# Dilated scores of a head pair on the two row halves of the TensorE array, three products of 64 rows each, instead of two stacked products of 128 rows

## The chip, the cores and the metric

The kernel runs on one core of a Trainium2 chip. A core has a matrix engine (TensorE, called PE in the profile; its weight loads are listed apart as PEld), a vector engine (DVE), a scalar engine (ACT), a general engine (POOL) and a queue engine that issues most transfers (SP). Each engine works through its own instructions in the order in which the program lists them, and they wait for one another by semaphores. The metric is the device time of one execution in microseconds (us), smaller being better; the number of a version is the median of several executions.

## What is computed

Two layers of an encoder over 1024 tokens of width 1024. Layer 0 is latent attention, layer 1 is dilated window attention; each is followed by an MLP. The change touches the dilated attention alone: 16 heads of 64 dimensions in three groups with (window, dilation) of (128, 1), (512, 4) and (2048, 16). For each group and head the reference does this:

```python
q = rms_norm(proj[:, :, gi, 0], g_q[gi])
k = rms_norm(proj[:, :, gi, 1], g_k[gi])
...
s = jnp.einsum('nbqhd,nbkhd->nbhqk', qb, kb,
               preferred_element_type=jnp.float32) * (DIL_HEAD_DIM ** -0.5) + bias
s = jnp.where(valid[None, :, None], s, -jnp.inf)
lse = jax.nn.logsumexp(s, axis=-1)
p = jnp.exp(s - lse[..., None]).astype(v.dtype)
o = jnp.einsum('nbhqk,nbkhd->nbqhd', p, vb)
```

The scores s of a block of 128 queries against its 256 neighbouring keys are a product over 64 dimensions. The kernel makes float32 accuracy out of a shorter format (F32R in the code): every operand is split into a high part and a remainder, hi and lo, and the product becomes a sum of products of parts.

## The kernel before

The dilated stage (function `dil`) walks through steps of 128-row tile pairs: for each of three groups g and eight head pairs pr, four steps tp, each of which takes two tiles of 128 tokens. A loop at the end of `dil` calls the parts of a software pipeline in turn. In one step it projects the tile pair tp (`project`, 24 products of 128x256 for each tile, on the lines 414 to 416 of the helper `mm3`), normalizes it (`qkstep`), transposes an earlier pair and splits it into hi and lo (`stacks`), computes scores for two tiles that are ready (`scores`), transposes the weights of two earlier tiles (`ptrans`) and multiplies two others with the values (`av`). Program order is only the starting point: the framework simulates the program and writes each engine's list in the order in which its model of durations finds the instructions ready.

`stacks` (L1832) transposes the queries and keys of both heads into one PSUM bank psq: 128 rows, 64 of each head. For head e it then writes a stack into the tile kT: hi on the head's own 64 rows (ACT, L1846) and lo on the other 64 rows (DVE, L1847). The tile has one such 128-row plane for each head. For the queries it needs the stack in swapped order too, lo above hi, and gets it by two transfers on SP's queue into the tile qs (L1850).

`scores` (L1860) thus needs two products of all 128 rows for a head: stack times stack gives hi·hi + lo·lo, swapped stack times stack gives lo·hi + hi·lo. That is four products of 128x256 for the two heads of a tile (L1873), all into the two halves of one PSUM bank pss. DVE adds the bias tile bt and takes the row maximum (L1878, once a head), ACT makes the offset dnb (L1882) and the exponential into the tile pd (L1884). The PSUM pool of the stage has eight banks, handed out in turn.

Before the stage there is one place to which the prediction turns: the table of bias values is built with nine products of only 32 rows (L1444, in the function `bias_even`), and the latent attention multiplies weights with values on L870 to L872, with 66, 64 and 66 columns of the array.

Of the kernel before, what the change touches and what calls it, by code (L numbers as in the profile page):

```python
# [9 lines left out]
F32 = mybir.dt.float32  # L10
F32R = mybir.dt.float32r
# [3 lines left out]
AF = mybir.ActivationFunctionType  # L15
ALU = mybir.AluOpType
# [4 lines left out]
P = 128  # L21
D = 1024
S = 1024
# [18 lines left out]
class K:  # L42
# [1702 lines left out]
    def dil(self, at0, at1, tail, wqk, vd):  # L1745


        nc, a, tc = self.nc, self.a, self.tc
# [4 lines left out]
        D_ = lambda name, shape, dt, bufs: dpool.tile(list(shape), dt, tag=name, bufs=bufs, name=self.nm(name))  # L1753
        PS = lambda name, dt=F32: psp.tile([P, 512], dt, tag="b", name=self.nm(name))
# [12 lines left out]
        def project(h, w, ps, i, t):  # L1767
            tl = slice((t % 4) * P, (t % 4 + 1) * P)
            for d in range(ND):
                self.mm3(ps[:, i * 256 : (i + 1) * 256], h[t // 4](0, d)[:, tl], h[t // 4](1, d)[:, tl],  # L1770
                         w[d // 4][0][:, d % 4, :], w[d // 4][1][:, d % 4, :], d == 0, d == ND - 1)
# [60 lines left out]
        def stacks(u, tp, qn):  # L1832

            ps = PS("psq")
            for k in range(2):
                for i in range(2):
                    c = i * 256 + (1 - k) * P
                    nc.tensor.transpose(ps[:, (2 * k + i) * P : (2 * k + i + 1) * P], qn[:, c : c + P], self.ident)
            q0 = S + tp % 2 * 256
            qs = D_("qs", (P, 2, 256), F32R, 3)  # L1840
            for e in range(2):
                n, m = (slice(64 * x, 64 * x + 64) for x in (e, 1 - e))
                s1 = 4 + tp % 2
                pair = lambda r: u["k"][r, e, :].rearrange("p (s x) -> p s x", x=256)[:, tp : s1 + 1 : s1 - tp, :]
                x = ps[n, :].rearrange("p (k x) -> p k x", k=2)
                nc.scalar.activation(pair(n), x, AF.Copy)  # L1846
                nc.vector.tensor_tensor(pair(m), x, pair(n).bitcast(F32), op=ALU.subtract)  # L1847
            for r in range(2):
                n, m = (slice(64 * x, 64 * x + 64) for x in (r, 1 - r))
                nc.sync.dma_start(out=qs[n].bitcast(F32), in_=u["k"][m, :, q0 : q0 + 256].bitcast(F32))  # L1850
            for i in range(2):
                u["q"][2 * tp + i] = (u["k"][:, :, q0 + i * P : q0 + (i + 1) * P], qs[:, :, i * P : (i + 1) * P])

        def span(g, t):
            if g == 2:
                return 64, 192
            n = 8 if g == 0 else 2
            return 64 if t % n == 0 else 0, 192 if t % n == n - 1 else 256

        def scores(u, t):  # L1860
            g, pr = u["g"], u["pr"]
            bt = D_("bt", (P, 2, 256), F32, 3)
            idx = self.even * (8 - t) + t
            src = self.bias[g][bass.ds(idx, 1), 2 * pr : 2 * pr + 2, 0 : P * 256]
            b0, b1 = (64, 192) if g == 2 else (0, 256)
            nc.sync.dma_start(out=bt[:, :, b0:b1], in_=src.rearrange("o h (q c) -> q (o h) c", c=256)[:, :, b0:b1])
            ps = PS("pss")
            w0 = min(max(P * t - 64, 0), S - 256)
            off = w0 - (P * t - 64)
            q = u["q"].pop(t)  # L1870
            for e in range(2):
                for k in range(2):
                    nc.tensor.matmul(ps[:, e * 256 : (e + 1) * 256], q[k][:, e, :], u["k"][:, e, w0 : w0 + 256],  # L1873
                                     start=k == 0, stop=k == 1)
            lo, hi = span(g, t)
            p = D_("pd", (P, 2, 256), F32, 4)
            for e in range(2):
                nc.vector.tensor_tensor_reduce(  # L1878
                    p[:, e, lo:hi], ps[:, e * 256 + lo - off : e * 256 + hi - off], bt[:, e, lo:hi], op0=ALU.add, op1=ALU.max,
                    scale=1.0, scalar=-3.0e38, accum_out=stat[:, g, t, 0, 2 * pr + e : 2 * pr + e + 1])  # L1880
            nb = self.sm("dnb", 2)
            nc.scalar.activation(nb, stat[:, g, t, 0, 2 * pr : 2 * pr + 2], AF.Identity, scale=-1.0, bias=ln14)  # L1882
            for e in range(2):
                nc.scalar.activation(p[:, e, lo:hi], p[:, e, lo:hi], AF.Exp, bias=nb[:, e : e + 1],  # L1884
                                     accum_out=stat[:, g, t, 1, 2 * pr + e : 2 * pr + e + 1])
            if g < 2:
                if lo:
                    nc.gpsimd.memset(p[:, :, 0:lo], 0)
                if hi < 256:
                    nc.gpsimd.memset(p[:, :, hi:256], 0)  # L1890
            return p
# [138 lines left out]
        def fetch(n):  # L2030
            if n in firsts:
                loads[n] = self.dil_weights(*firsts[n][1:3])

        def fetch_split(n):
            if n in firsts:
                wts[firsts[n][0:3]] = loads.pop(n)()
# [43 lines left out]
        transposed, scored, ready, carry, stacking, stk, late, after = [], [], [], [], None, [], [], None  # L2080
# [6 lines left out]
        for n, step in enumerate(steps):  # L2087
            fetch(n + 2)
            for f in vtodo.pop(n, ()):
                f()  # L2090
            if step is None and perms:
                while perms:
                    permute(*perms.pop(0))
                HT = new
                h = [(lambda k, d, t=t: t[k][d // 2][:, d % 2, :]) for t in HT]
            if step is not None and n + 1 < len(steps) and steps[n + 1] is None and step[1] < 2:
                new = [[[], []], [[], []]]
                perms = [(step[1] + 1, dp, k) for dp in range(4) for k in range(2)]
                for _ in range(2):
                    permute(*perms.pop(0))  # L2100
            w = None
            if step is not None:
                kind, g, pr, tp = step
                w = wts[(kind, g, pr)]
                if tp == 0:
                    units[(g, pr)] = {"g": g, "pr": pr, "q": {}, "V": VSs[(g, pr // 2)],
                                      "k": D_("kT", (P, 2, S + 512), F32R, 2), "U": self.G("U", (P, 8, P), F32)}
                u = units[(g, pr)]
            for x in transposed:
                x[0]["at"] = n  # L2110
                av(*x)
            fetch_split(n + 1)
            if step is not None:
                ps = PS("psproj")
                project(h, w, ps, 0, 2 * tp)
            transposed = [(u_, t_, ptrans(u_, t_, p_)) for u_, t_, p_ in scored]
            for u_, t_, _ in scored:
                if u_["g"] == 2:
                    if u_["pr"] < 7:
                        if t_ == 7:  # L2120
                            um(u_, (0, 1))
                    elif t_ in (1, 5):
                        um(u_, (t_ // 4,))
            scored = [(u_, t_, scores(u_, t_)) for u_, t_ in ready]
            ready, carry = carry, []
            stk.append(stacking)
            if len(stk) > 1:
                x = stk.pop(0)
                if x is not None:
                    stacks(*x)  # L2130
                    u_, tp_ = x[:2]
                    ready = ready + ([(u_, 2 * tp_ - 1), (u_, 2 * tp_)] if tp_ else [(u_, 0)])
                    carry = [(u_, 7)] if tp_ == 3 else []
            late, merged[:] = late + merged, []
            while late and (step is None or late[0][1] < n):
                u_, _, ths = late.pop(0)
                emit(u_, ths)
            if step is not None:
                project(h, w, ps, 1, 2 * tp + 1)
                if step == ("qk", 2, 7, 3):  # L2140
                    tail()
                    after = n + 1
            if n == after:
                for pp in range(3):
                    self.reload(O, src, pp, 0, nc.sync)
            stacking = None
            if step is not None:
                stacking = (u, tp, qkstep(u, tp, ps))
# [163 lines left out]
```

## Time and profile before

| | us |
|---|---|
| median of 3 executions | 3348.64 |
| lowest and highest | 3348.17, 3349.63 |
| the profiled execution, its own time | 3350.56 |
| span of its instructions | 3348.8 |
| first and last product of L1873 in the span | 1692.2 to 2618.2 |

The mean granted TensorE clock was 0.981. A row of the timeline gives an instruction's start and its duration, both in us from the start of the span; a group row gives count, busy time and mean duration in ns, and then the idle time of that engine just before these instructions with what ended it. Products overlap: a product of 128x256 is listed with some 0.28 us though the next one starts 0.12 us later. So the engine's pace is read from the distance of the starts, not from the durations, and a busy PE need not be at its best pace.

### The profile page before, as it was taken

What the parts mean: (1) busy time and instruction counts of PE and PEld (TensorE: products, weight loads), DVE (VectorE), ACT (ScalarE), POOL (GpSimd) and SP (SyncE); (2) the same over time, 40 slices, a digit from 0 to 9 for tenths busy, and PEclk for the clock granted to TensorE, in tenths of its full rate; (3) what the DMA queues carried; (4) which work ended last, traced back from release to release, by engine and by line L of the source; (5) the groups of instructions that cost most, each with busy time, mean ns of one, the idle gap of its engine ahead of it and who ended that gap; (6) DMA issues with size and microseconds to landing.
All of it is one profiled execution on the core that took longest, in us unless ns stands there. A gap on an engine that the chain in (4) does not pass through costs nothing. (4 is left out here: it accounts for less than half of the span.)

```text
span 3348.8 us, 52027 instructions
## 1 busy us (share of the span) xinstructions
PE 3201.8 (96%) x18278; PEld 2737.9 (82%) x18278; DVE 2521.1 (75%) x4491; ACT 1810.8 (54%) x3606; POOL 749.9 (22%) x1077
## 2 busy tenths in 40 slices
PE   6999999999999999899999989998898899999999
PEld 6877677678888788778899989998888688887887
DVE  5677777747877856787678888888899578778666
ACT  5547777735444434542257776677566245444342
POOL 6455565520111000001122222222111001110000
PEclk9999999999999999999999999999999799999999
DMA  5453232243655797546445545544455725439564
GB/s 186 130 170 96 91 103 84 86 157 108 214 185 188 263 283 233 168 143 206 166 121 143 139 125 143 150 133 128 131 146 150 225 85 198 154 128 320 199 198 129
DMA packets 412948, 536.39 MB, mean 160 GB/s; under 512 B 40677, under 2 KB 295058, under 8 KB 412682
## 3 DMA queue, kind: packets, MB, share of 16 engines
q1 hardware_dynamic: 385322, 441.70, 43.2%
q0 software_dynamic: 27360, 91.31, 7.3%
q8 instruction: 146, 2.39, 0.3%
q14 instruction: 120, 0.98, 0.1%
HBM read 376.17 MB, written 132.62 MB: 152 GB/s over the span
## 5 line engine op out<-in xcount | busy, mean ns | idle before, releaser
L415 PE MATMUL psm<-dl,dh 128*128 128x512 f32 x896 | 351.0, 392 | 9.2 <-DVE dl L122 9.1
L414 PE MATMUL psm<-hf,wf 128*128 128x512 f32 x896 | 349.6, 390 | 2.6 <-ACT wf L121 2.5
L416 PE MATMUL psm<-dh,dl 128*128 128x512 f32 x896 | 350.2, 391 | 0.0
L415 PE MATMUL psm<-hf,wf 128*128 128x512 f32 x896 | 348.8, 389 | 0.0
L416 PE MATMUL psm<-hf,wf 128*128 128x512 f32 x896 | 346.7, 389 | 0.4 <-DVE wf L122 0.4
L414 PE MATMUL psm<-dh,dh 128*128 128x512 f32 x896 | 335.1, 391 | 6.1 <-ACT dh L121 6.1
L414 PE MATMUL psproj<-wqkh,hTp 128*128 128x256 f32 x1024 | 301.4, 294 | 1.6 <-DVE stat L1878 1.6
L416 PE MATMUL psproj<-wqkh,hTp 128*128 128x256 f32 x1024 | 291.8, 285 | 0.0
L415 PE MATMUL psproj<-wqkl,hTp 128*128 128x256 f32 x1024 | 291.1, 284 | 0.0
L1829 POOL TENSOR_TENSOR qn<-qn,dgain 128x256 f32<-128x256 f32 x96 | 83.5, 870 | 596.0 <-DVE qn L1827 494.2
L121 ACT ACTIVATE dh<-ufr 128x1024 fp32r<-128x1024 f32 x112 | 118.3, 1056 | 178.5 <-PE psm L416 59.9
L415 PEld LDWEIGHTS psm<-dl,dh 128*128 128x128 f32 x896 | 169.3, 189 | 47.3 <-DVE dl L122 12.0
L414 PEld LDWEIGHTS psm<-dh,dh 128*128 128x128 f32 x896 | 168.2, 188 | 43.1 <-ACT dh L121 8.4
L414 PEld LDWEIGHTS psm<-hf,wf 128*128 128x128 f32 x896 | 168.2, 188 | 39.8 <-ACT wf L121 5.5
L414 PEld LDWEIGHTS psproj<-wqkh,hTp 128*128 128x128 f32 x1024 | 196.4, 192 | 1.9 <-issue 1.9
L416 PEld LDWEIGHTS psm<-hf,wf 128*128 128x128 f32 x896 | 168.2, 188 | 36.2 <-DVE wf L122 1.2
L416 PEld LDWEIGHTS psm<-dh,dl 128*128 128x128 f32 x896 | 169.1, 189 | 35.1
L415 PEld LDWEIGHTS psproj<-wqkl,hTp 128*128 128x128 f32 x1024 | 196.7, 192 | 0.0
L415 PEld LDWEIGHTS psm<-hf,wf 128*128 128x128 f32 x896 | 168.2, 188 | 34.4
L416 PEld LDWEIGHTS psproj<-wqkh,hTp 128*128 128x128 f32 x1024 | 196.2, 192 | 0.0
L122 DVE TENSOR_TENSOR dl<-ufr,dh 128x1024 fp32r<-128x1024 f32 x112 | 136.9, 1222 | 76.5 <-ACT dh L121 57.7
L745 DVE TENSOR_REDUCE mx<-pmx 128x1 f32<-128x512 f32 x256 | 165.1, 682 | 29.5 <-PE pmx L743 29.4
(397 smaller groups left out, 9398.9 us busy)
## 6 DMA issues: line engine op xcount, KB each, us to landing
ufr<-uf SPq DMA_DIRECT2D x112, 512.0 KB
adaw<-in_ada_w SPq DMA_DIRECT2D x96, 512.0 KB
w2r<-in_mlp_w SPq DMA_DIRECT2D x96, 512.0 KB
w1r<-in_mlp_w SPq DMA_DIRECT2D x64, 512.0 KB
bt<-bias SPq DMA_DIRECT2D x128, 256.0 KB
wqkr<-in_dil_w_in SPq DMA_DIRECT2D x96, 256.0 KB
qs<-kT SPq DMA_DIRECT2D x192, 128.0 KB
qkv<-st SPq DMA_DIRECT2D x32, 512.0 KB
```

What stands on the lines that cost most here:

```text
L121: nc.scalar.activation(hi, src, AF.Copy)
L122: (lo_eng or nc.vector).tensor_tensor(lo, src, hi.bitcast(F32), op=ALU.subtract)
L414: mm(out, lh, rh, start=first, stop=False)
L415: mm(out, lh, rl, start=False, stop=False)
L416: mm(out, ll, rh, start=False, stop=last)
L745: nc.vector.tensor_reduce(maxes[h][:, 2 * j + b : 2 * j + b + 1], ps, op=ALU.max, axis=AX.X)
L1829: nc.gpsimd.tensor_tensor(qq, qq, gain[:, g : g + 1, :].unsqueeze(1).broadcast_to([P, 2, 2, 64]), op=ALU.mult)
```

## The change

Queries and keys of both heads are split in place: plane 0 of kT holds hi and plane 1 holds lo, each with head 0 on rows 0 to 63 and head 1 on rows 64 to 127. One ACT and one DVE instruction of 128 rows do it where there were two of 64 rows each; the tile qs and its two transfers are gone. The scores of a head are then three products of 64 rows (hi·hi, lo·hi, hi·lo; lo·lo is left out), on the half of the array's rows on which the head lies. The code lists them in turn, one of head 0, one of head 1. The two heads go to two PSUM banks; the two tiles of a step share these, each in its half of the columns.

```diff
@@ stacks
-            q0 = S + tp % 2 * 256
-            qs = D_("qs", (P, 2, 256), F32R, 3)
-            for e in range(2):
-                n, m = (slice(64 * x, 64 * x + 64) for x in (e, 1 - e))
-                s1 = 4 + tp % 2
-                pair = lambda r: u["k"][r, e, :].rearrange("p (s x) -> p s x", x=256)[:, tp : s1 + 1 : s1 - tp, :]
-                x = ps[n, :].rearrange("p (k x) -> p k x", k=2)
-                nc.scalar.activation(pair(n), x, AF.Copy)
-                nc.vector.tensor_tensor(pair(m), x, pair(n).bitcast(F32), op=ALU.subtract)
-            for r in range(2):
-                n, m = (slice(64 * x, 64 * x + 64) for x in (r, 1 - r))
-                nc.sync.dma_start(out=qs[n].bitcast(F32), in_=u["k"][m, :, q0 : q0 + 256].bitcast(F32))
+            s1 = 4 + tp % 2
+            hi, lo = (u["k"][:, k, :].rearrange("p (s x) -> p s x", x=256)[:, tp : s1 + 1 : s1 - tp, :] for k in range(2))
+            x = ps.rearrange("p (k x) -> p k x", k=2)
+            nc.scalar.activation(hi, x, AF.Copy)
+            nc.vector.tensor_tensor(lo, x, hi.bitcast(F32), op=ALU.subtract)
             for i in range(2):
-                u["q"][2 * tp + i] = (u["k"][:, :, q0 + i * P : q0 + (i + 1) * P], qs[:, :, i * P : (i + 1) * P])
+                c = S + (tp % 2 * 2 + i) * P
+                u["q"][2 * tp + i] = u["k"][:, :, c : c + P]
@@ scores
-        def scores(u, t):
+        def scores(u, t, pss, i):
...
-            ps = PS("pss")
...
-            for e in range(2):
-                for k in range(2):
-                    nc.tensor.matmul(ps[:, e * 256 : (e + 1) * 256], q[k][:, e, :], u["k"][:, e, w0 : w0 + 256],
-                                     start=k == 0, stop=k == 1)
+            for n, (a, b) in enumerate(((0, 0), (1, 0), (0, 1))):
+                for e in range(2):
+                    r = slice(64 * e, 64 * e + 64)
+                    nc.tensor.matmul(pss[e][:, i * 256 : (i + 1) * 256], q[r, a, :], u["k"][r, b, w0 : w0 + 256],
+                                     start=n == 0, stop=n == 2)
...
-                    p[:, e, lo:hi], ps[:, e * 256 + lo - off : e * 256 + hi - off], bt[:, e, lo:hi], op0=ALU.add, op1=ALU.max,
+                    p[:, e, lo:hi], pss[e][:, i * 256 + lo - off : i * 256 + hi - off], bt[:, e, lo:hi], op0=ALU.add, op1=ALU.max,
@@ the loop over the steps
-            scored = [(u_, t_, scores(u_, t_)) for u_, t_ in ready]
+            scored = []
+            for k, (u_, t_) in enumerate(ready):
+                if k % 2 == 0:
+                    pss = [PS("pss") for _ in range(2)]
+                scored.append((u_, t_, scores(u_, t_, pss, k % 2)))
```

What the two programs list for the engines differs beyond the diff, since the lists come out of the framework's simulation. On PE, in the first group, the scores of a step before (pspt are transposed weights, pss the scores, psq the transposes of `stacks`; what stands in brackets is the engine whose semaphore the row waits for):

```order
L1899 MATMUL pspt_21874<-ident,pd_21754 128x128
L1873 MATMUL pss_21884<-kT_21261 128x256 [waits DVE_49,PE_49]
L1873 MATMUL pss_21884<-kT_21261,qs_21611 128x256
L1873 MATMUL pss_21884<-kT_21261 128x256 [waits DVE_49]
L1873 MATMUL pss_21884<-kT_21261,qs_21611 128x256
L1873 MATMUL pss_21898<-kT_21261 128x256 [waits PE_49]
L1838 MATMUL psq_21910<-ident,qn_21654 128x128 [waits PE_49]
```

The first tile has its four products in a row, and the first product of the second tile follows at once in a bank of its own. The other three follow six projection products later and wait for the two transfers into qs.

The first tile of the same step in the changed program, on PE:

```order
L1893 MATMUL pspt_21863<-ident,pd_21748 128x128
L1867 MATMUL pss_21871<-kT_21254 128x256 [waits DVE_49]
L1867 MATMUL pss_21872<-kT_21254 128x256 [waits DVE_49]
L1867 MATMUL pss_21871<-kT_21254 128x256
L1867 MATMUL pss_21872<-kT_21254 128x256
L1867 MATMUL pss_21871<-kT_21254 128x256
L1867 MATMUL pss_21872<-kT_21254 128x256
L1838 MATMUL psq_21903<-ident,qn_21644 128x128 [waits DVE_49]
```

Its six products alternate between the heads (banks 21871 and 21872), as the code lists them. The second tile comes 22 projection products later:

```order
L414 MATMUL psproj_21830<-wqkh_21677,hT_3879_18986 128x256
L1867 MATMUL pss_21871<-kT_21254 128x256 [waits DVE_49]
L1867 MATMUL pss_21871<-kT_21254 128x256 x2
L1867 MATMUL pss_21872<-kT_21254 128x256 [waits DVE_49]
L1867 MATMUL pss_21872<-kT_21254 128x256 x2
L415 MATMUL psproj_21830<-wqkl_21678,hT_3879_18986 128x256
```

It writes the same two banks and waits for DVE, which reads the first tile's scores from them. Its products do not alternate: three of head 0, then three of head 1. Over the whole stage the 1152 products stand in 257 unbroken runs between products of 128 rows. With a and b for the two heads these are: 45 times ababab, 60 times aaabbb, 22 times aabbab, 4 times babab, 29 times abab, 23 times aba, 23 times bab, 29 times ab, 9 times aaa, 9 times bbb and 4 times a. Of the 257 runs, 48 are followed by a product of `av`, the others by products in 32-bit formats.

## The prediction

> **What bounds the kernel now.** I read the page's first lines, then the busy time by stretches of the dilated stage, then the groups of the lines that the diff touches with their waits, and last the timeline at the places where the array's division changes.
>
> ```profile
> span 3348.8 us, 52027 instructions
> PE 3201.8 (96%) x18278; PEld 2737.9 (82%) x18278; DVE 2521.1 (75%) x4491; ACT 1810.8 (54%) x3606; POOL 749.9 (22%) x1077
> ```
>
> PE has work in flight for 96% of the span. By stretches, which cover nearly all of the stage's scores (two of 50 us are the borders between groups):
>
> ```profile
> core 0: us, PE busy (x) PEld busy (x) DVE busy (x) ACT busy (x) POOL busy (x), PEclk, DMA share, GB/s
> 1700.00:1950.00 250.00, 245.79 (x2226) 242.60 (x2226) 207.60 (x535) 179.13 (x485) 53.15 (x78) 1.00 0.51 139
> 1950.00:2000.00 50.00, 40.13 (x352) 39.00 (x350) 44.33 (x99) 37.77 (x86) 18.16 (x21) 0.90 0.46 121
> 2000.00:2250.00 250.00, 248.11 (x2254) 245.85 (x2254) 203.53 (x544) 175.97 (x491) 59.77 (x122) 1.00 0.53 144
> 2250.00:2300.00 50.00, 41.26 (x357) 40.33 (x356) 44.34 (x104) 39.42 (x100) 15.71 (x26) 0.90 0.40 108
> 2300.00:2550.00 250.00, 230.34 (x1960) 224.94 (x1959) 218.57 (x613) 155.39 (x483) 49.06 (x54) 0.97 0.51 140
> ```
>
> In the first two groups PE stands still for only 4.2 and 1.9 of 250 us, with DVE at 83% and 81%: PE sets the pace, and every slot on it counts. In the third group PE is idle for 19.7 us of 250 while DVE is busy for 87%; there DVE's work and some transfers count too. So the change is worth what it does to PE's slots, plus some relief in the third group.
>
> The distance between the starts of products is the price of a slot:
>
> ```profile
> 2006.23 0.28 PE L1873 MATMUL pss<-kT,qs 128*128 128x256 f32 x1
> 2006.23 0.19 PEld L1873 LDWEIGHTS pss<-kT 128*128 128x128 f32 x1
> 2006.34 0.28 PE L1873 MATMUL pss<-kT 128*128 128x256 f32 x1
> 2006.46 0.28 PE L1873 MATMUL pss<-kT,qs 128*128 128x256 f32 x1
> 2006.58 0.28 PE L416 MATMUL psproj<-wqkh,hTp 128*128 128x256 f32 x1
> 2006.87 0.35 DVE L1878 CUSTOM_DVE_ANT_0 pd<-pss,bt 128x192 f32<-128x192 f32 x1
> ```
>
> Three steps in 0.35 us: 0.12 us a product. The next weight load starts together with the running product, so the load hides behind it.
>
> **The change part by part. Slots.** Before, 4 products for each of 192 tiles: 768 slots, 92.2 us. Now there are 1152 products of 64 rows. How much they cost depends on two things that no row of this trace shows for 64 rows: whether a product on the lower rows runs beside one on the upper rows, and what it costs to divide the array. If neighbours run side by side, a run aaabbb takes five slots (the products are issued in order, so only the last a has a b beside it), ababab three, aabbab four. Over the 257 runs: 45×3 + 60×5 + 22×4 + 4×3 + 29×2 + 46×2 + 29×1 + 18×3 + 4×1 = 772 slots, +0.5 us. If they don't, it is 1152 slots, 138.2 us, +46 us. That all tiles alternate would be 576 slots and -23 us, but the list on PE rules it out: the second tile of a step waits bank by bank for DVE and mostly stands as aaabbb. I take side by side: the two halves share neither rows nor bank, and the rows above show that load and stream already overlap. But it is not shown, and 46 stays in the range.
>
> **Dividing the array.** The trace has one place where products of fewer rows stand between products of 128: the bias table, nine products of 32 rows with 129 columns.
>
> ```profile
> 1164.98 0.39 PE L416 MATMUL psm<-dh,dl 128*128 128x512 f32 x1
> 1165.29 0.51 PEld L1444 LDWEIGHTS <-tabw 32*128 32x128 bf16 x9 [0.35 <-issue]
> 1165.30 0.68 PE L1444 MATMUL psb<-oh,tabw 32*128 32x129 bf16 x9
> ...
> 1165.76 0.21 PE L1444 MATMUL psb<-oh,tabw 32*128 32x129 bf16 x1
> 1165.91 0.19 PEld L414 LDWEIGHTS psm<-dh,dh 128*128 128x128 f32 x1
> 1165.91 0.50 PE L414 MATMUL psm<-dh,dh 128*128 128x512 f32 x1
> 1166.01 0.19 PEld L415 LDWEIGHTS psm<-dl,dh 128*128 128x128 f32 x1
> 1166.25 0.39 PE L415 MATMUL psm<-dl,dh 128*128 128x512 f32 x1
> 1166.25 0.19 PEld L416 LDWEIGHTS psm<-dh,dl 128*128 128x128 f32 x1
> 1166.48 0.40 PE L416 MATMUL psm<-dh,dl 128*128 128x512 f32 x1
> ```
>
> On the way in, the load doesn't start with the running product at 1164.98 but 0.31 us later, with no semaphore that explains it ("issue"). The pace of these products is 0.23 (1166.25 to 1166.48), so the load is held 0.08 beyond the slot. On the way out the last of the nine starts at 1165.76, its slot is 0.06 (eight steps from 1165.30), and the load comes at 1165.91: held 0.09. The load that was held is then no longer hidden: the product behind it truly starts where the next load does, 0.10 later (1165.91 to 1166.01). A 32-bit load thus costs about 0.18 on the way in and 0.19 on the way out, 0.37 a run; before a 16-bit product the 0.10 falls away (1165.29 to 1165.30).
>
> There is a counterexample, columns in place of rows:
>
> ```profile
> 277.54 0.39 PE L870 MATMUL pav<-ph,hv 128*66 128x512 f32 x1
> 277.55 0.14 PEld L871 LDWEIGHTS pav<-ph,hv 128*64 128x64 f32 x1
> 277.78 0.40 PE L871 MATMUL pav<-ph,hv 128*64 128x512 f32 x1
> 278.01 0.39 PE L872 MATMUL pav<-pl,hv 128*66 128x512 f32 x1
> ```
>
> From 66 columns to 64 and back the pace stays 0.24 and 0.23: no cost. So the price of a run lies between 0 and 0.37 us. I take 0.37, since L1444 is the nearest case: it cuts the rows, as the change does, while L871 cuts the columns and starts at column 0, and so may be no more than a narrow case of all 128. 257 × 0.37 = 95, less 48 × 0.10 for the runs before a 16-bit product: +90 us, or 0 at the other end.
>
> The Trainium skill, "TensorEngine Tiling (Array Packing)", section Tiling Modes, Key Properties, says that a change of the tiling mode, unlike a change of tile, drains the engine, and that different tiles load and multiply in parallel. The 32-row place agrees with the first (0.37 us there and back); the 64-column place does not, though that page lists 128×64 as a mode of its own. By the rule the sum is the one forecast here; without it, it is the rival named second. That tiles run in parallel no run here shows.
>
> **Splits and stacks.**
>
> ```profile
> L1847 DVE TENSOR_TENSOR kT<-psq,kT 64x512 fp32r<-64x512 f32 x192 | 132.2, 688 | 23.8 <-ACT kT L1846 18.3
> L1846 ACT ACTIVATE kT<-psq 64x512 fp32r<-64x512 f32 x192 | 113.2, 590 | 46.1 <-PE psq L1838 29.2 <-DVE kT L1847 11.0 <-issue 2.5
> L1902 DVE TENSOR_TENSOR pT<-pspt,pT 128x512 f16<-128x512 f32 x128 | 87.5, 687 | 15.4 <-ACT pT L1901 14.1
> L1901 ACT ACTIVATE pT<-pspt 128x512 f16<-128x512 f32 x128 | 71.8, 592 | 51.5 <-PE pspt L1899 49.8 <-PE psav L1915 1.3
> L1873 PE MATMUL pss<-kT,qs 128*128 128x256 f32 x384 | 108.7, 301 | 15.6 <-DMA qs<-kT 15.2
> ```
>
> 128 rows take as long as 64 on both engines (687 against 688 ns, 592 against 590), so half of the instructions falls away: 66 us of DVE and 57 us of ACT. In the first two groups this lies beside PE's work and is worth nothing. In the third, DVE is relieved of 0.69 us in each of 32 steps, 22 us, against PE's 19.7 us of idle time; part of that belongs to transfers, and what DVE gives free another wait can take. I take -10, between 0 and -16.
>
> The 192 transfers into qs go, from the crowded queue of SP and from the path. PE waited 15.2 us for them (last row). What is late next there is lo out of DVE, which those transfers had to wait for as well: -15, with 0 as the other end.
>
> **A new wait.** The second tile writes the banks from which DVE reads the first. DVE's first reading ends at 2007.22, that is 0.76 after the start of the last product at 2006.46; the list puts 22 projection products, 2.6 us, in between. Behind the waiting product stand projections, for which in turn `qkstep` waits. How late DVE's maxima come shows in ACT's wait for them:
>
> ```profile
> ACT dnb L1882 <- DVE stat L1878: 56.5, 51, 3.6
> ```
>
> 1.1 us on average over 51 waits, 3.6 at most: mostly inside the cover of 2.6. The lower end is 0; the upper, if all 51 were as long as the longest, 51 × 1.0 = +51. I take +5, near the average.
>
> **Sum.** Against the profiled execution's own 3350.56: +0.5 (slots) +90 (division) -15 (qs) -10 (third group) +5 (banks) = +70.5, so 3421. That execution lies 1.9 over the median of the runs shown, so I forecast 3419 for a median.
>
> **The rivals.** All on the same base.
> - Neither half runs beside the other, and the division costs its 0.37: +46 +90 -15 -10 +5 = +116, 3465. For it: nothing shows two products at once. Against it: nothing shared is known between the halves but the path of the loads.
> - The division costs nothing, as with the 64 columns, and the halves run side by side: +0.5 -15 -10 +5 = -19.5, 3329. This is the faster side; it holds as long as a run's division costs less than 19.5 / 257 = 0.076 us. For it speak the rows of L870 to L872, against it those of L1444.
> - No cost of division, but one half after the other (the change then doesn't do what its words say): +46 -15 -10 +5 = +26, 3375.
> - DVE decides: division free and side by side, but the second tile's wait is at its upper end: +0.5 -15 -10 +51 = +26.5, 3375. For it: DVE over 80% busy. Against it: the 2.6 us of cover.
>
> The Trainium skill, "TensorE: Matmul & The Clock Gate", Part 3: Packing small matmuls, The mechanism, puts the start of a neighbouring tile some 4 ns after the first; by that the slots are the 772 counted here. No run here shows it.
>
> **How the numbers follow.** Forecast 0.40, one after the other with division 0.20, free and side by side 0.24, free but one after the other 0.11, DVE 0.05. Some 0.2% (6.7 us) is what a measurement of this kernel can tell from no change. Faster by more: the third case, 0.24 less a little that ends near zero, 0.23; within: 0.04, out of the edges of the third and fourth; slower: 0.73. The range leaves out half of the second case (above 3465) and a bit less than half of the third (below 3327): 3327 to 3465. The forecast's own range, with 0.3 us a run and the third group's relief at 16 on one side, 0.4 us and both gains at 0 on the other, is 3390 to 3452.
>
> **What would show it.** Side by side: in a run ababab the starts of a and b lie closer than 0.02 us, pairs 0.12 apart; one after the other: all 0.11 to 0.12 apart. Division: the first weight load of a run starts some 0.2 us after the product before, not with it, and the load behind the run as well. The bank wait: an idle time of PE before L1867 that DVE's pd of L1872 ends, over 10 us in total. The relief: PE idle in the third group clearly under 19.7 us. I am wrong if the loads at a run's edges start with the product before: then the sum falls to 3329 or 3375.

## The result, and the profile after

| | before | after |
|---|---|---|
| median, us (executions of each on one chip) | 3349.14 (4) | 3381.38 (4) |
| lowest and highest | 3348.17, 3356.16 | 3379.87, 3388.24 |
| the profiled execution | 3350.56 | 3381.33 |
| span of its instructions | 3348.8 | 3379.4 |

The change makes the kernel slower by 32 us: the ratio is 1.0096, with an interval from 1.0076 to 1.0115. The forecast was 3419 and slower by 70; the result lies in the full range of the prediction, 3327 to 3465, and below the narrower one that it gives for its own case, 3390 to 3452.

The page of the changed kernel begins with the span and with each engine's busy time, its share and its number of instructions:

```profile
span 3379.4 us, 52008 instructions
...
PE 3262.6 (97%) x18662; PEld 2732.9 (81%) x18662; DVE 2440.0 (72%) x4395; ACT 1751.2 (52%) x3510; POOL 750.5 (22%) x1077
```

The 384 added products are there (18662 against 18278), DVE has 81 us less to do and ACT 60. By the same three stretches as before:

```profile
core 0: us, PE busy (x) PEld busy (x) DVE busy (x) ACT busy (x) POOL busy (x), PEclk, DMA share, GB/s
1700.00:1950.00 250.00, 250.00 (x2203) 228.82 (x2201) 175.09 (x476) 151.82 (x429) 49.84 (x73) 1.00 0.37 106
2000.00:2250.00 250.00, 249.85 (x2218) 230.55 (x2216) 172.02 (x478) 146.41 (x427) 55.90 (x110) 1.00 0.38 106
2300.00:2550.00 250.00, 239.27 (x2021) 217.19 (x2020) 196.44 (x577) 146.85 (x456) 55.28 (x66) 0.98 0.39 112
```

In the first two groups PE stands still for less than 0.2 us of 250 and DVE is busy for about 70%: PE sets the pace more plainly than before. In the third its idle time fell from 19.7 to 10.7 us. Where the 32 us lie shows from a mark that every version has: ACT squares a projection (L1822) 32 times in each group. From the first to the last of the 32 starts it takes, in us worked out from the traces:

```
group                first   second   third
before               285.8   289.8    288.2
after                300.7   309.3    287.9
difference           +14.9   +19.5    -0.3
```

All of the loss is in the two groups that PE bounds. In the third, something gives back what the products cost.

The timeline at a run of six half-row products that the list on PE has as aaabbb (a for a product of head 0 on the upper rows, b for one of head 1 on the lower):

```profile
2011.09 0.28 PE L414 MATMUL psproj<-wqkh,hTp 128*128 128x256 f32 x1
2011.29 0.42 PEld L1867 LDWEIGHTS pss<-kT 64*128 64x128 f32 x6
2011.30 0.62 PE L1867 MATMUL pss<-kT 64*128 64x256 f32 x6
2011.85 0.19 PEld L415 LDWEIGHTS psproj<-wqkl,hTp 128*128 128x128 f32 x1
2011.85 0.39 PE L415 MATMUL psproj<-wqkl,hTp 128*128 128x256 f32 x1
...
2011.96 0.19 PEld L416 LDWEIGHTS psproj<-wqkh,hTp 128*128 128x128 f32 x1
2012.07 0.28 PE L416 MATMUL psproj<-wqkh,hTp 128*128 128x256 f32 x1
```

Two things are to be seen. The first load of the run comes 0.20 us after the product before it (2011.09 to 2011.29) instead of with it, and the load after the run comes with its product (both at 2011.85), so nothing hides it. And six products fit between 2011.30 and 2011.85. The single starts, as medians over the runs of six in the trace whose first two lie about 10 ns apart, stand at 0, 10, 223, 233, 341 and 351 ns: three pairs. (Where the list has ababab the first two lie 3 ns apart.) A pair 10 ns apart can't be two products of one half, whose starts lie some 0.12 apart, so each a has a b beside it although the list has all three a ahead of the first b. (The trace doesn't name the half; this is inferred from the distances.)

The view of the tile pss answers how long its users stood still and until what; two of its lines bear on the prediction, the second being all of the bank wait:

```profile
  issue: 23.8, 115
...
  DVE stat L1872: 0.8, 3
```

Last, the groups of the split and, from the list of waits in the stage (total us, times, longest), ACT's wait for the maxima:

```profile
L1843 DVE TENSOR_TENSOR kT<-psq,kT 128x512 fp32r<-128x512 f32 x96 | 65.8, 686 | 6.5 <-ACT kT L1842 5.8
L1842 ACT ACTIVATE kT<-psq 128x512 fp32r<-128x512 f32 x96 | 57.2, 596 | 46.8 <-PE psq L1838 46.8
```

```profile
ACT dnb L1876 <- DVE stat L1872: 33.8, 34, 3.2
```

The split takes half of what it took (132.2 and 113.2 us before), and ACT waits 33.8 us for DVE's maxima where it was 56.5.

### The profile page after: what moved, and what is told of

Same layout as the page of the kernel before. It is cut to its first block, busy times and chain, and to the rows that moved or that the text cites. A ratio compares the mean times of both kernels' runs of the same rounds, so it can differ in the third digit from the quotient of the medians.

```text
span 3379.4 us, 52008 instructions
## 1 busy us (share of the span) xinstructions
PE 3262.6 (97%) x18662; PEld 2732.9 (81%) x18662; DVE 2440.0 (72%) x4395; ACT 1751.2 (52%) x3510; POOL 750.5 (22%) x1077
## 4 chain that ended last, share of the span: by engine, by line
PE 83%; DVE 5%; issue 3%; DMA 3%; POOL 2%; ACT 2%; SPq 1%; DVEq 0%; POOLq 0%; ACTq 0%
PE psm L415 11%; PE psm L416 11%; PE psm L414 11%; PE psproj L414 5%; PE psproj L415 5%; PE psproj L416 5%; PE pss L1867 3%; PE pspt L1893 2%; PE psv L415 2%; PE psv L416 2%; PE psv L414 2%; PE psy L414 2%; PE psy L415 2%; PE psy L416 2%; PE psq L1838 2%
## 5 line engine op out<-in xcount | busy, mean ns | idle before, releaser
L1872 DVE CUSTOM_DVE_ANT_0 pd<-pss,bt 128x192 f32<-128x192 f32 (+2 forms) x384 | 121.4, 348 | 104.1 <-PE pss L1867 99.5
```

The source lines that it names most:

```text
L1872: nc.vector.tensor_tensor_reduce(p[:, e, lo:hi], pss[e][:, i * 256 + lo - off : i * 256 + hi - off], bt[:, e, lo:hi], op0=ALU.add, op1=ALU ...
```

## The experiments

Every kernel ran beside the kernel before on the same chip, whose median there was 3348.3, 3347.8 or 3349.4. The framework lists every kernel anew, so an edit can change the order on other engines' lists too; where that bears on a reading it is said. The theories bear the letters that the expectations give them. A diff is against the changed kernel unless its first line names another. A pinned instruction keeps the place on its engine's list at which the program writes it.

### Both tiles' products in one run

```diff
@@ the loop of dil
+            pss = [PS("pss") for _ in range(2)] if ready else None
+            for k, (u_, t_) in enumerate(ready):
+                products(u_, t_, pss, k)
             for k, (u_, t_) in enumerate(ready):
-                if k % 2 == 0:
-                    pss = [PS("pss") for _ in range(2)]
-                scored.append((u_, t_, scores(u_, t_, pss, k % 2)))
+                scored.append((u_, t_, scores(u_, t_, pss, k)))
```

`products` issues the six products that stood in `scores`, pinned. On PE's list the 257 runs of the changed kernel become 99, of which 93 have twelve products abababababab; if a run takes as many slots as its longer half has products, 630 slots become 576.

> The changed kernel, with the six products of both tiles of a step listed together and kept in that order (ababab ababab), DVE's readings behind them: 99 unbroken runs instead of 257, 576 slots if the halves run side by side. Theory A (what costs is dividing the array: some 0.35 us for every run, whatever is in it; the halves go on independently, and in the third group other work sets the pace so that PE's extra slots cost nothing there): 158 runs and 54 slots less are 55 + 6 us over the stage, of which two thirds are seen: 3381 - 40 = 3341, between 3332 and 3350. Theory B (products are issued in order across the halves, 772 slots, and division costs less): 196 slots less, 3381 - 24 = 3357. Theory C (the second tile's wait for DVE on the shared banks costs the 32 us): 3349.

Measured: 3316.79 us (3313.23 to 3319.81), ratio to before 0.990 with an interval from 0.9885 to 0.9918. It is 65 us under the changed kernel and faster than both. The timeline of one run:

```profile
2013.81 0.60 PE L1896 MATMUL pspt<-ident,pd 128*128 128x128 f32 x4
...
2014.34 0.77 PEld L1860 LDWEIGHTS pss<-kT 64*128 64x128 f32 x12 [0.17 <-issue]
2014.34 0.98 PE L1860 MATMUL pss<-kT 64*128 64x256 f32 x12
...
2015.25 0.42 PEld L1838 LDWEIGHTS psq<-ident,qn 128*128 128x128 f32 x4
2015.25 0.66 PE L1838 MATMUL psq<-ident,qn 128*128 128x128 f32 x4
```

Twelve products from 2014.34 to 2015.25, with one held load on each side. The starts, as medians over the 93 runs of twelve, are at 0, 3, 223, 226, 341, 344, 466, 469, 579, 583, 698 and 702 ns: six slots. The direction of A is right, its size too small: the whole saving came, not two thirds of it. That a run has a price of its own is likely after this but not shown, since the joined list also moves other work.

### The same with the heads in blocks

The joined list with all six a ahead of all six b: `for e in range(2)` goes from inside `products` to outside the loop over the tiles. The runs stay, only the order in them changes.

> As the joined kernel, but with all six products of head 0 listed first and then all six of head 1 (aaaaaabbbbbb), some 100 runs. Theory A (halves independent of the list's order): six slots a run as before, same time as the joined kernel within 5 us, and in the trace the first b starts less than 0.05 us after the first a. Theory B (issued in order): the first b starts with the sixth a, eleven slots a run, 5 x 0.12 x 92 = +55 us over the stage, some +37 seen against the joined kernel.

Measured: 3347.17 us (3342.88 to 3350.67), 30 us over the joined kernel. A had said that the order doesn't matter; that fails. The run:

```profile
2018.41 1.11 PEld L1859 LDWEIGHTS pss<-kT 64*128 64x128 f32 x12 [0.17 <-issue]
2018.41 1.32 PE L1859 MATMUL pss<-kT 64*128 64x256 f32 x12
...
2019.66 0.42 PEld L1838 LDWEIGHTS psq<-ident,qn 128*128 128x128 f32 x4
```

It takes 1.25 us up to the next load (2018.41 to 2019.66) where the joined one took 0.91. The median starts are at 0, 223, 341, 348, 466, 571, 579, 691, 698, 808, 928 and 1048 ns: three pairs and six single ones, nine slots. The first b comes with the third a. Three slots more in 93 runs are 3 × 0.118 × 93 = 33 us. So the halves do run independently of the list, but a product can overtake only some of those listed ahead of it.

### Blocks of four

To test that, the joined list as a a a a b b b b a a b b.

```diff
@@ the loop of dil, against the joined kernel
-            for k, (u_, t_) in enumerate(ready):
-                products(u_, t_, pss, k)
+            listed = [(u_, t_, j_, n_) for j_, (u_, t_) in enumerate(ready) for n_ in range(3)]
+            for piece in (listed[:4], listed[4:]):
+                for e_ in range(2):
+                    for u1, t1, j_, n_ in piece:
+                        products(u1, t1, pss, j_, e_, (n_,))
```

> The joined list in blocks of four: a a a a b b b b a a b b. Theory A (a product starts as soon as its half of the rows is free, as long as no more than three or four products listed ahead of it still wait): the first b starts within 20 ns of a1 or a2 and the run stays at six or seven slots, so 3317 to 3328. Rival B (only the last product of a block of one half runs beside the first of the next, as the six-block list showed with its b1 beside a3 or later): nine slots, 93 x 3 x 0.118 = 33 us more, 3350.

Measured: 3319.84 us (3314.41 to 3320.5), 3 over the joined kernel, within both runs' spread.

```profile
2010.17 0.78 PEld L1860 LDWEIGHTS pss<-kT 64*128 64x128 f32 x12 [0.17 <-issue]
2010.18 0.99 PE L1860 MATMUL pss<-kT 64*128 64x256 f32 x12
...
2011.09 0.42 PEld L1838 LDWEIGHTS psq<-ident,qn 128*128 128x128 f32 x4
```

0.92 us and six pairs; the second start, which by the distances is the first b, stands 13 ns behind the first although four a are listed ahead of it. B falls. A block of four costs nothing, one of six costs three slots. The starts tell the reach more closely. Here the first b passes three a that have not begun (the second to the fourth). In blocks of six it doesn't start beside the second a at 223 ns, when four a are still to begin, but beside the third at 348 ns, when three are. So a product passes three that have not begun, and not four. Which start belongs to which half is again inferred from the distances.

### No division of the array

```diff
@@ scores, against the changed kernel
-            for n, (a, b) in enumerate(((0, 0), (1, 0), (0, 1))):
-                for e in range(2):
-                    r = slice(64 * e, 64 * e + 64)
-                    nc.tensor.matmul(pss[e][...], q[r, a, :], u["k"][r, b, w0 : w0 + 256], start=n == 0, stop=n == 2)
+            for e in range(2):
+                for n, (a, b) in enumerate(((0, 0), (1, 1 - e))):
+                    nc.tensor.matmul(pss[e][...], q[:, a, :], u["k"][:, b, w0 : w0 + 256], start=n == 0, stop=n == 1)
```

Everything of the change stays except the halves: four products over all rows for a tile, 768 slots as before.

> The changed kernel with four products of all 128 rows for each tile instead of six of 64 (it mixes the two heads in the products, so the scores are not the reference's): no division, 768 slots as before the change, and yet no stacks, no transfers into qs, half the split instructions, shared banks with the wait for DVE. Theory A: the cost of division goes and what the change saved stays: 3349 - 15 (qs) - 10 to -18 (third group) = 3316 to 3326. Theory C (shared banks): the wait is still there, 3370 to 3381. Theory B with cheap division: 768 slots for 772, 3375 to 3381.

Measured: 3317.67 us (3314.47 to 3323.41), as A said; B and C fall. This splits the change in two. The halved split, the missing transfers and the shared banks together are worth 3317.67 - 3348.32 = -31 us, and the half-row products cost 3381.38 - 3317.67 = +64 in spite of fewer slots. The relief is mostly in the third group: 266.9 us between its marks, 21 less than before.

### A run cut in two

```diff
@@ the loop of dil, against the joined kernel
             transposed = [... for u_, t_, p_ in scored[:1]]
+            held = scored[1:]
...
             for k, (u_, t_) in enumerate(ready):
                 products(u_, t_, pss, k)
+                if k == 0:
+                    transposed += [(u1, t1, ptrans(u1, t1, p1, True)) for u1, t1, p1 in held]
```

The same instructions; four transposes change their place on PE.

> The joined list again, but in every step the four transposes of the second tile's probabilities stand between the two tiles' products: nothing is added or left out, the run of twelve becomes two of six, 191 runs in place of 99, 576 slots as before. Theory A (each division of the array costs about 0.35 us there and back, by the offsets, about 0.31 by the time of the full-row kernel): 92 x 0.31 to 0.35 = 29 to 32 us over the joined kernel's 3316.8, so 3346 to 3349, and two held weight loads in each step. Rival R (a division costs little by itself, and the joined list won by removing waits elsewhere): within 5 us of 3317. A price of a half, 15 us or 3332, would say that other work covers part of each.

Measured: 3346.35 us (3344.38 to 3350.71), 29.6 over the joined kernel: 29.6 / 92 = 0.32 us for a run. A hits, R falls. One half of a cut run:

```profile
2009.68 0.60 PE L1896 MATMUL pspt<-ident,pd 128*128 128x128 f32 x4
2010.21 0.41 PEld L1860 LDWEIGHTS pss<-kT 64*128 64x128 f32 x6 [0.17 <-issue]
2010.21 0.62 PE L1860 MATMUL pss<-kT 64*128 64x256 f32 x6
...
2010.76 0.42 PEld L1838 LDWEIGHTS psq<-ident,qn 128*128 128x128 f32 x4
```

Each cut has its own held load of 0.17 us ahead and its unhidden load behind. The list of groups counts these over the whole kernel, the joined one first, then the cut one (busy time, mean ns, idle time before):

```profile
L1860 PEld LDWEIGHTS pss<-kT 64*128 64x128 f32 x1152 | 76.6, 190 | 16.7 <-issue 12.6 <-PE pspt L1896 1.3 <-DVE drt L115 0.7
```

```profile
L1860 PEld LDWEIGHTS pss<-kT 64*128 64x128 f32 x1152 | 82.3, 190 | 33.0 <-issue 28.6 <-PE pspt L1896 2.7 <-PE psproj L415 0.3
```

The idle time ahead of the loads grows by 16.3 us, that is 0.18 for each of 92 runs; the rest of the 0.32 is on the way out. This is the cleanest price in the study, as nothing was added or left out. The order on other engines' lists did change (of DVE's 683 instructions between the marks of the third group, 622 still stand in the same order), but the distances on PE give the same price without them: from the last transpose ahead of a run to the second product behind it, the median run of six takes 917 ns here and the run of twelve 1276 in the joined kernel. Two of six less one of twelve, less two transposes of 0.109 by which these stretches differ, are 0.34 us.

### The joined list without division

The product loop of the full-row kernel in the joined list (768 products, none of half the rows).

> The joined list with four products over all 128 rows a tile (768 in all, no division of the array) in place of six of 64; as they mix the two heads of a pair, the scores are not those of the reference. Theory A (a division costs 0.32 us, as cutting the joined run showed, and a slot 0.117): from the joined kernel's 3316.8, less 99 x 0.32 = 32, plus 192 x 0.117 = 22: 3307, within 5. It would also say that listing the tiles together saves some 10 us by itself, against the full-row kernel's 3317.7. Rival R (the price of a division is less where it stands once a step, or a pair of half-row products costs more than a slot): 3315 to 3320.

Measured: 3316.40 us (3315.53 to 3318.43), the same as joined with halves. By the total R is right: on top of the full-row products the 99 divisions and the 192 saved slots nearly cancel, and joining the tiles saves nothing by itself. But the run itself is as A priced it:

```profile
2016.53 1.20 PE L1859 MATMUL pss<-kT 128*128 128x256 f32 x8
2017.46 0.46 PEld L1838 LDWEIGHTS psq<-ident,qn 128*128 128x128 f32 x4
2017.56 0.60 PE L1838 MATMUL psq<-ident,qn 128*128 128x128 f32 x4
```

From the last transpose ahead to the second product behind, the median run takes 1172 ns here and 1276 with halves: eight slots and no division against six and one, so a division is 104 + 2 × 118 = 340 ns. In the first two groups, where PE decides, the halves are 5.4 us longer between the marks (570.4 against 565.0), near 66 × 0.104 = 6.9. The third group is 6.8 shorter with halves; why, stays open.

### The copies alone

```diff
@@ stacks, against the joined kernel
+            xa, xd = (D_(f"extra{k}", (P, 2, 256), F32, 1) for k in range(2))
+            nc.scalar.activation(xa[0:64], x[0:64], AF.Copy)
+            nc.vector.tensor_tensor(xd[0:64], x[0:64], hi[0:64].bitcast(F32), op=ALU.subtract)
```

As many instructions of ACT and DVE as before the change, without a reader.

> As the joined kernel, with one more ACT and one more DVE instruction of 64 x 512 in every step, whose results nobody reads: the work that the change took from these engines is given back to them, 96 x 0.69 us of DVE and 96 x 0.59 us of ACT; 109 runs instead of 99, which alone is +2 to +4. Theory A (DVE is what sets the pace of the third group): first two groups unchanged within 5 us, third group longer by 10 to 22 us. Rival (the third group is set by something else, such as transfers): no group changes by more than 5 us.

Measured: 3327.02 us (3326.96 to 3327.18), 10.2 over the joined kernel; by the marks the third group is 10.4 longer, the first -1.6 and the second +1.3. But PE's products stand in 109 runs here instead of 99, and all ten more lie in the third group: at 0.32 us they are 3 of the 10, so some 7 are left for the copies and for the order of DVE's list, which changed there too (541 of 683 instructions in the same order). The copies cost where DVE is at work for most of the time, and nothing that shows where PE decides.

### The transfers alone

Three kernels. The first is the kernel before without the transfers:

```diff
@@ stacks, against the kernel before
-            qs = D_("qs", (P, 2, 256), F32R, 3)
...
-            for r in range(2):
-                n, m = (slice(64 * x, 64 * x + 64) for x in (r, 1 - r))
-                nc.sync.dma_start(out=qs[n].bitcast(F32), in_=u["k"][m, :, q0 : q0 + 256].bitcast(F32))
             for i in range(2):
-                u["q"][2 * tp + i] = (u["k"][:, :, ...], qs[:, :, ...])
+                u["q"][2 * tp + i] = (u["k"][:, :, ...],) * 2
```

> The kernel before without the two transfers per step: its second two products read the first tile in place of the swapped one, so its scores are not those of the reference; the four products over all rows, the four 64-row copies and one bank a tile stay. If the relief of the full-row kernel (about 31 us) was 10 us of copies, as the joined kernel with two extra copies showed, and the rest transfers, this one is 15 to 21 us under before: 3327 to 3333, mostly in the third group. If the transfers were hidden: within 4 us of 3348.

Measured: 3330.06 us (3328.78 to 3334.37), 17.8 under before, as expected; by the marks -5.7, -2.8 and -11.3 in the three groups. Here too the lists changed, DVE's in the third group most (512 of 704 in the same order). The second is the joined kernel with the transfers of the kernel before put back into a tile without a reader:

```diff
@@ stacks, against the joined kernel
+            q0 = S + tp % 2 * 256
+            qs = D_("qs", (P, 2, 256), F32R, 3)
+            for r in range(2):
+                n, m = (slice(64 * x, 64 * x + 64) for x in (r, 1 - r))
+                nc.sync.dma_start(out=qs[n].bitcast(F32), in_=u["k"][m, :, q0 : q0 + 256].bitcast(F32))
```

> The joined kernel with the two transfers per step of the kernel before put back, into a tile that nothing reads: their traffic and their issues without anybody waiting for their end. If the relief of the third group came from the transfers' own load on SyncE's queue and the DMA engines, its span grows by 5 us or more and the time is 3322 to 3330. If it came from products no longer waiting for the transfers to land, or from the halved copies on ScalarE and VectorE alone, nothing changes: 3314 to 3320.

Measured: 3332.09 us (3330.2 to 3333.21), 15.3 over the joined kernel, of which 11.9 in the third group. That is a little over the upper end named. So the transfers cost nearly as much without anybody waiting for them as with. The third takes away their bytes:

```diff
@@ stacks, against the kernel with unread transfers
-                n, m = (slice(64 * x, 64 * x + 64) for x in (r, 1 - r))
+                n, m = (slice(64 * x, 64 * x + 4) for x in (r, 1 - r))
```

> The joined kernel with two unread transfers per step again, at the same places of SyncE's list and with the same waits, but of 4 rows each in place of 64, 16 KB a step in place of 256 KB. If the 15 us that the unread transfers cost come from their bytes (the DMA engines, and with them the landing of um and bt in the third group), nearly all of it goes: 3316 to 3321. If they come from SyncE's queue (its issue time and its wait for VectorE's lo, ahead of the issues of bt behind them), it stays: 3328 to 3333.

Measured: 3331.66 us (3329.82 to 3333.26), the same. DVE's lists of these two kernels agree (679 of 683 instructions in the third group), so it isn't the bytes. What reaches PE, from the waits between 2300 and 2620 us, for the joined kernel:

```profile
ACT dnb L1879 <- DVE stat L1875: 16.6, 16, 3.1
PEld pspt L1896 <- ACT pd L1881: 7.9, 12, 3.3
...
PE pspt L1896 <- ACT pd L1881: 5.1, 4, 3.1
DVE um L1981 <- DMA um<-U: 3.6, 3, 1.8
```

and with the small transfers (line numbers five higher):

```profile
ACT dnb L1884 <- DVE stat L1880: 36.6, 22, 4.9
...
PEld pspt L1901 <- ACT pd L1886: 19.5, 16, 5.2
PE pspt L1901 <- ACT pd L1886: 16.1, 7, 5.0
DVE um L1986 <- DMA um<-U: 6.9, 7, 3.1
```

PE waits longer for ACT's weights (+11.0 us in this window) and ACT longer for DVE's row maxima (+20.0). Between the marks of the third group alone, which is 13.7 us longer, PE's own wait for the weights grows by 7.0 (0.4 to 7.4), about half. The chain is read from the waits; no run isolates its links. Why the maxima come later isn't shown. It looks as if DVE stood waiting for um, which goes out and comes back on SyncE's queue (3.6 to 6.9 us), but with the transfers of full size, which cost as much, DVE waits for um for only 2.9 us.

There is a second candidate beside SyncE's queue: the order on DVE's list. In the first two groups the joined kernel and both kernels with transfers have DVE's instructions in the same order (but for one at a border), and there the transfers cost at most 2.7 us in all. In the third, only 599 and 596 of 683 still stand in the joined kernel's order, and there is the loss. Whether it comes from the transfers in the queue or from the list that the framework writes for a program with transfers, the runs don't separate.

## Why the prediction was wrong

The forecast was +70.5, the result +32.2. Of the range that the prediction gives for its own case, the lower end, 3390, comes out as 3395 from the two changes named for it (18 and 6 under 3419); the result is under both. Term by term, with what the runs give for each:

| term | forecast | measured | from |
|---|---|---|---|
| slots | +0.5 | -16.3 | 630 slots for 768, at 0.118 |
| dividing the array | +90 | +82 | 257 × 0.32, the cut run |
| transfers into qs | -15 | -17.8 | the kernel before without them |
| halved split, third group | -10 | -7 to -10 | the added copies, without and with their ten more runs |
| bank wait | +5 | +0.8 | the tile view after |
| sum | +70.5 | +38.5 to +42 | |

Here 257 × 0.32 = 82 and (630 - 768) × 0.118 = -16.3. The last three terms together, -24 to -27, were -31 in the full-row kernel; with that figure the sum is 35. So the measured prices come out 3 to 10 over the 32.2 measured. They were taken in different surroundings, with lists written anew, and this rest stays unexplained.

**Slots: the step that failed.** "The products are issued in order, so only the last a has a b beside it", hence five slots for aaabbb and 772 in all. The premise was mine and no row showed it. In the changed kernel aaabbb has three slots (starts at 0, 10, 223, 233, 341 and 351 ns); over the 257 runs that makes 630 (637 by the starts in the trace, where three runs of six take longer). The 17 us between are nearly half of the miss. The limit is a reach, not the order: it takes blocks of six (+30 us) to lose slots, while blocks of four lose none. That each engine works through its instructions in the order listed, as is said ahead of the prediction, thus doesn't hold for these products. The Trainium skill, "TensorE: Matmul & The Clock Gate", Part 3, The mechanism, says both that a neighbouring tile starts some 4 ns later, with which the 3 to 4 ns of the alternating list agree, and that products start strictly in the order of the program; with the second the pairs of aaabbb differ, and the measurement decides.

**Dividing the array: right, a little too large.** 0.37 us a run from nine products of 32 rows in the bias table, 0.32 in the cut run, 0.34 between the single runs with and without halves. On 257 runs the difference to the forecast is 8 us. The signs named for it are there: the load 0.20 us late ahead of the run, the load behind it unhidden. The rule of the page "TensorEngine Tiling (Array Packing)" of the Trainium skill, section Tiling Modes, Key Properties, that a change of mode drains the engine, agrees with this price at 64 rows; the place with 64 columns, on which the third case rested, was no guide to it.

**Transfers: the size right by luck, the reason not.** The prediction read the 15.2 us that PE waited for qs as the gain. The gain measured is 17.8, but 15.3 of such a cost also come where no product waits for a transfer. What PE's row showed is thus not what was gained; the main part falls in the third group and comes of SyncE's queue or of the order of DVE's list, which the runs don't separate. "From the crowded queue of SP" stood in the text, without a price.

**The third group: right in size.** -10 forecast, 7 to 10 by the added copies. PE's idle time there did fall (19.7 to 10.7 us in the stretch), as named, but the missing transfers and PE's own longer work lower it as well, so this sign doesn't prove the size.

**The bank wait: too large.** 0.8 us in three places; the list's 22 projection products cover it nearly always. The rival in which DVE decides falls with it, and so do those with one half after the other (the pairs) and those with free division (the held loads).

## What to carry to other kernels

Half-row products on the two halves of the array do run beside each other, but each run of them between full-row products costs 0.32 us here, there and back, nearly three slots of 0.118: count the runs, not only the products, and gather the half-row products into few long runs. With 99 runs in place of 257 the same change becomes a gain, 3316.8 us against 3349 before. That gain comes from what the change drops beside the products, the copies and transfers (-31 us in the full-row kernel): against full-row products in the same list, which mix the heads and give no usable scores (3316.4), the half-row products break even.

Transfers of 8 KB cost as much here as transfers of 128 KB, and as much without a reader as with one. So a transfer's price can't be read from its bytes or from the wait of its reader alone. Whether it came here from the place in SyncE's queue or from the order of DVE's list is not settled.

## What was not expected of the hardware

Products on one half overtake products of the other that are listed ahead: three that have not begun (first pair 13 ns apart with four a ahead of the first b), and not four (with six a ahead, the first b comes 348 ns late, beside the third a). In each run of halves the first slot is long, 223 ns to the second start of a half, and those after it 0.11 to 0.13; in the full-row run behind a transpose it is 200 ns too, so the division shows itself in the 0.20 us ahead of the run and in the load behind it, not there. What sets this reach no run here tells.
